# Bias bands read backwards from one 30 KB table, and four PSUM banks for products outside the attention

## The chip, the cores and the metric

The kernel runs on one core of a Trainium2 chip. Such a core has five engines that work side by side, each through its own list of instructions in order: TensorE (PE in the profile, its weight loads PEld), VectorE (DVE), ScalarE (ACT), GpSimd (POOL) and SyncE (SP), and 16 DMA engines that all queues share. The metric is the device time of one execution in microseconds, as the median of several runs. Lower is better.

## The reference, cut to what matters

A trunk of two layers works on 256 positions of 1024 columns, all in float32. Each layer adds half of a gated FFN (2816 wide), an attention of three branches whose gated results are summed and projected, half of a second FFN, and a last gated term.

```
for i in range(DEPTH):
    h = h + 0.5 * swiglu(rms_norm(h, g0), ffn1_wi[i], ffn1_wo[i])
    n = rms_norm(h, g1); q, k, v, gates of the branches = split_cols(n @ w_in[i], IN_SPLITS)
    ya = diff_attention(...)         # 4 heads of two score maps each, causal
    yb = nsa_attention(...)          # 8 heads: compressed blocks, selected blocks, window
    yc = swa_sink_attention(...)     # 8 heads, window of 128, with sinks
    h = h + (sum of sigmoid(gate) * (y @ w_branch)) @ w_out[i]
    h = h + 0.5 * swiglu(rms_norm(h, g2), ffn2_wi[i], ffn2_wo[i])
    h = h + sigmoid(rms_norm(h, g3) @ w_ple_gate[i]) * (p[i] @ w_ple[i])
return rms_norm(h, final_norm)
```

All three branches add a bias to the scores that depends on the distance between query and key alone: `rel_bias[rel_bucket(dist)]`, one column for each of 20 heads, with 32 buckets for distances up to 128. Where a key may not be seen, the score is -1e30.

## The kernel before, in words

Each product of float32 matrices is made of three matmuls of a shorter format: a left side and a weight are each split into a high part and the rest (`mul3`, lines 220 to 222: high by high, high by rest, rest by high). Weights come as a stream of chunks of 128 x 1024 (512 KB). SyncE fetches a chunk into one of four `raw` buffers (line 263), ScalarE copies it to the high part `wh` (line 213), and VectorE subtracts to get the rest, `wl` (line 208). Six buffers hold split chunks. A chunk of an FFN product covers two of the eight 128-row steps of the sum.

A product (`product`, lines 290 to 305) runs over two halves of 128 positions, t = 0 and 1, with one PSUM bank each (128 x 512), the second half some steps behind the first. When a half is done its `done` function empties the bank. The program writes the work in this order, and a scheduler then places the instructions of each engine by priority and by its own idea of time; buffers and banks that share a tag (`mm`, `s`, `tp`, `y`) are handed out in turn, and an instruction that needs one waits until the last reader of its previous content is done.

The eight banks are: two `mm` for products, two `s` for attention scores, three `tp` for transposes, one `y`.

In the first FFN of the program there are 11 products of gate and up columns (tiles ff; in the order the third is ff_354 and ff_406 before, ff_353 and ff_405 after). `done` applies Silu on ScalarE (line 458) and multiplies on VectorE into `gated` (line 459): after that the bank is free. Every second product the result is cut into 16-bit halves (`cut`, line 426), turned by DMA (`flip`, line 427), put together (`whole`, line 432) and split (gT).

Beside this FFN the program makes its constants (`setup`). One matmul and an addition give `tb`, the bias of 20 heads at 384 distances, with -1e30 where the mask forbids (line 1060). GpSimd writes it to `table` in DRAM (line 1061) and copies it 128 times, to `rev` (line 1062). A band is a tile of 128 queries x 4 heads x 256 distances in which each query's row is shifted by one place; `rev_band` reads it with a row step of one element less than a row of `rev` (line 1035). GpSimd reads two bands for the compressed branch, from which eight small copies make `cbias` (lines 1086 and 1087); SyncE reads five bands a layer for the attention. There line 529 adds a band to the scores and takes the maximum in one VectorE instruction:

```
nc.vector.tensor_tensor_reduce(out=p[j], in0=ps[j], in1=bias[j], scale=-1.0, scalar=low,
                               op0=ALU.add, op1=ALU.min, accum_out=st[:, j:j + 1])
```

Of the kernel before, what the change touches and what calls it, by code (L numbers as in the profile page):

```python
# [134 lines left out]

def _constants():
    u = np.arange(REV)
    dist = 255 - u
    n = np.maximum(dist, 0)
    nf = np.maximum(n, 1).astype(np.float32)  # L140
    big = 16 + (np.log(nf / np.float32(16)) / np.float32(math.log(MAXDIST / 16)) * np.float32(16)).astype(np.int32)
    bucket = np.where(n < 16, n, np.minimum(big, BUCKETS - 1))
    onehot = (bucket[None, :] == np.arange(BUCKETS)[:, None]).astype(np.float32)
    dead = np.zeros((NB, REV), np.float32)
    dead[:, dist < 0] = NEG
    dead[12:, dist >= 128] = NEG
    ql, t, m = np.arange(128)[:, None, None], np.arange(2)[None, :, None], np.arange(16)[None, None, :]
    cmask = ((128 * t + ql - 16 * m - 31 >= 0) & (m < 15)).astype(np.float32).reshape(128, 32)
    return {"onehot": onehot, "dead": dead, "cmask": cmask, "ident": np.eye(128, dtype=np.float32),
            "fold": np.tile(np.eye(32, dtype=np.float32), (2, 1))}  # L150
# [28 lines left out]
def trunk(ctx: ExitStack, tc: tile.TileContext, a: dict, out: bass.AP, index: list):  # L179
# [10 lines left out]

    def mm_bank(name):
        return bank("mm", 2, name)

    def tp_bank(name):
        return bank("tp", 3, name)
# [94 lines left out]
    def product(lhs, nk, done, name, w, skew=SKEW):  # L290

        def run():
            ps = [None] * NT
            for step in range(nk + skew):
                for t, k in ((0, step), (1, step - skew)):
                    if 0 <= k < nk:
                        wh, wl = w(k)
                        if k == 0:
                            ps[t] = mm_bank(f"{name}{t}")
                        xh, xl = lhs(t, k)  # L300
                        mul3(ps[t][:, :w.width], xh, xl, wh, wl, k == 0, k == nk - 1)
                        if k == nk - 1:
                            done(t, ps[t])
                        flow.tick()
        return run
# [182 lines left out]
    def attention(i, norm, after):  # L488
# [3 lines left out]
        def begin():  # L492
            nonlocal pool
            pool = phase("attn")
            for t in range(NT):
                merged[t] = pool.tile([128, D], F32, name=f"merged{t}")

# [56 lines left out]

        def band(first):
            b = pool.tile([128, 4, 256], F32, tag="band", bufs=2, name="band")
            rev_band(b, first)
            return b

        def y_tile(name):  # L560
# [20 lines left out]
        def attend_a():  # L581
            bnd = band(0)

            def first(u):
                m, t = u
                nk = 128 * (t + 1)
                s = scores("s", qk[m], [0, 1], t, lambda x, r, k: qk[m][r, x, 2 + k, :nk])
                yield
                p = pool.tile([128, 4, 256], F32, tag="p", bufs=3, name="p")
                st = None  # L590
                for st in softmax([p[:, j, :nk] for j in range(4)], [s[j // 2][:, j % 2, :nk] for j in range(4)],
                                  [bnd[:, 2 * m + j % 2, 256 - nk:] for j in range(4)]):
                    yield
                nc.vector.reciprocal(st[:, 8:12], st[:, 4:8])
                nc.vector.tensor_scalar(st[:, 10:12], st[:, 10:12], nlam[:, i:i + 1], None, op0=ALU.mult)
                for x in range(2):
                    nc.vector.tensor_scalar(p[:, 2 + x, :nk], p[:, 2 + x, :nk], st[:, 10 + x:11 + x], None, op0=ALU.mult)
                    nc.vector.scalar_tensor_tensor(p[:, x, :nk], p[:, x, :nk], st[:, 8 + x:9 + x], p[:, 2 + x, :nk],
                                                   op0=ALU.mult, op1=ALU.add)
                yield  # L600
                return p
# [191 lines left out]
        def attend_b():  # L793
            bnd, y_ps = {}, {}

            def first(u):
# [3 lines left out]
                if t == 0:  # L800
                    p = pool.tile([128, 4, 2, 128], F32, tag="p", bufs=3, name="p")
                    s = scores("s", qB[0], [2 * g, 2 * g + 1], 0, lambda x, r, m: kB[0][r, x, g:g + 3:2, :128])
                    rows = [(j, k) for j in range(4) for k in range(2)]
                    pr = [p[:, j, k] for j, k in rows]
                    sr = [s[j // 2].rearrange("p m (k n) -> p m k n", k=2)[:, j % 2, k] for j, k in rows]
                    br = [bnd[g][:, j, 128:] for j, k in rows]
                else:
                    p = pool.tile([128, 4, 256], F32, tag="p", bufs=3, name="p")
                    s = scores("s", qB[0], [2 * g, 2 * g + 1], 1, lambda x, r, m: kB[0][r, x, 2 * ss[0] + g, :])
                    pr = [p[:, j] for j in range(4)]  # L810
                    sr = [s[j // 2][:, j % 2] for j in range(4)]
                    br = [bnd[g][:, j] for j in range(4)]
                n = len(pr)
                yield
                st = None
# [48 lines left out]
        def attend_c():  # L864
# [4 lines left out]
            def first(u):  # L869
# [7 lines left out]
                sink = nsink[:, i, 4 * g:4 * g + 4]  # L877
                pr = [p[:, j, :nk] for j in range(4)]
                st = None
                for st in softmax(pr, [s[j // 2][:, j % 2, :nk] for j in range(4)], [bnd[g][:, j, 256 - nk:] for j in range(4)], sink):  # L880
                    yield
                sub(st[:, 8:12], st[:, 0:4], sink)
                nc.scalar.activation(st[:, 8:12], st[:, 8:12], AF.Exp)
# [89 lines left out]
        yield compress  # L973
        yield from branch(2, yC)
        yield from branch(1, yB, True)
        for c in range(2):
            yield product(lambda t, k: (mT[t][:, 0, k, :], mT[t][:, 1, k, :]), NK, after(c), "wo", streamed(i, f"wo{c}", 512))

# [46 lines left out]
    sg = base.tile([128, DEPTH], F32, name="sg")  # L1025
    cbias = base.tile([128, NT, 8, 16], F32, name="cbias")
    table = dram.tile([1, NB * REV], F32, name="table")
    rev = dram.tile([128, NB * REV], F32, name="rev")

    def rows(src, steps):  # L1030
        return bass.AP(tensor=src.tensor, offset=src.offset, ap=[[0, 128]] + steps)

    def rev_band(b, first, queue=nc.sync):
        ap = rev[:, :]
        queue.dma_start(b, bass.AP(tensor=ap.tensor, offset=ap.offset + first * REV + 127,
                                   ap=[[NB * REV - 1, 128], [REV, 4], [1, 256]]))

    def fetched_late(queue, *args):
        tc.keep_in_program_order(queue.dma_start(*args))
# [1 line left out]
    def setup(pool):  # L1041
# [17 lines left out]
        tb = pool.tile([NB, REV], F32, name="tb")  # L1059
        nc.vector.tensor_tensor(tb, tb_ps[:NB, :REV], dead, op=ALU.add)  # L1060
        nc.gpsimd.dma_start(table[0, :].rearrange("(n u) -> n u", n=NB), tb)
        nc.gpsimd.dma_start(rev, table.to_broadcast([128, NB * REV]))
        nc.gpsimd.memset(cbias, NEG)
        nc.vector.tensor_scalar(nsink, nsink, -1.0, None, op0=ALU.mult)
        lv = lamp.rearrange("p l (a b d) -> p (l a) b d", a=2, b=2)
# [11 lines left out]
        bands = []  # L1077
        for g in range(2):
            b = pool.tile([128, 4, 256], F32, tag="band", bufs=2, name="band")
            rev_band(b, 4 + 4 * g, nc.gpsimd)  # L1080
            bands.append(b.rearrange("p (par pr) c -> p par pr c", par=2))
        yield
        for g, b in enumerate(bands):
            for par in range(2):
                o = cbias.rearrange("p t (g pr par) n -> p t g par pr n", g=2, par=2)
                tc.keep_in_program_order(nc.vector.tensor_copy(o[:, 0, g, par, :, 0:7], b[:, par, :, 159:256:16]))
                tc.keep_in_program_order(nc.vector.tensor_copy(o[:, 1, g, par, :, 0:15], b[:, par, :, 31:256:16]))
        yield

    opened = []  # L1090
# [81 lines left out]
```

## Time and profile before

| | us |
|---|---|
| median of 3 runs (1371.64 to 1373.06) | 1372.09 |
| the profiled execution, its own time | 1372.78 |
| its span, first to last instruction | 1371.0 |
| TensorE busy (98%) | 1341.5 |
| VectorE busy (69%) | 944.7 |
| ScalarE busy (57%) | 779.4 |
| weight chunks of 512 KB, issue to landing, median | 4.4 |
| the copy rev<-table, 3840 KB | 18.3 |

The profile is of one execution. "Busy" counts the time in which an engine has an instruction under way, so a matmul that is followed closely by the next overlaps it and the sum says nothing on pace; the number of matmuls in a stretch does. A row's idle time is put down to what ended it. The wait of an engine matters where it delays the engine that ends last.

### The profile page before, as it was taken

The page shows a single profiled execution, that of the slowest core. Times are in us where ns is not written, and L with a number is a line of the kernel's source. Part 1 is how long each engine was busy: PE and PEld are TensorE (multiplying, and loading weights), DVE is VectorE, ACT ScalarE, POOL GpSimd, SP SyncE. Part 2 cuts the span into 40 slices and gives each one's busy share as a digit, 9 for nine tenths or more (in the row PEclk, how much of TensorE's full clock was granted, in tenths as well). Part 3 has the DMA queues.
Part 4 walks back from the last instruction along what each step waited for, and adds up shares of the span by engine and source line. Part 5 has one row for each costly group of instructions (what it writes and reads, how often), then busy time and mean ns, then how long its engine had stood idle before and what let it go on. Part 6 is the DMA issues. An engine that isn't in the chain of part 4 may idle for free.

```text
span 1371.0 us, 18293 instructions
## 1 busy us (share of the span) xinstructions
PE 1341.5 (98%) x6454; PEld 1098.2 (80%) x6454; DVE 944.7 (69%) x1779; ACT 779.4 (57%) x1378; POOL 19.0 (1%) x37
## 2 busy tenths in 40 slices
PE   8988999999999999999999999999999999999997
PEld 6766888887787788888888888888887778888886
DVE  7546656777886766766677665667697776776665
ACT  7435445668766455545665444566785656455454
POOL 0000000000000000000000000000000000000000
PEclk9999999999999999999999999999999999999999
DMA  8797757444653467775657885754547435777662
GB/s 306 199 265 227 216 177 237 142 152 156 215 175 109 153 189 213 215 210 192 203 189 219 223 226 171 235 170 137 162 151 232 127 122 168 216 222 218 194 202 84
DMA packets 121993, 261.07 MB, mean 190 GB/s; under 512 B 56816, under 2 KB 62372, under 8 KB 121774
## 3 DMA queue, kind: packets, MB, share of 16 engines
q1 hardware_dynamic: 121006, 254.34, 60.3%
q0 software_dynamic: 464, 5.01, 1.2%
q8 instruction: 50, 0.82, 0.2%
q10 hardware_dynamic: 432, 0.56, 0.1%
q14 instruction: 41, 0.34, 0.1%
HBM read 247.26 MB, written 5.01 MB: 184 GB/s over the span
## 4 chain that ended last, share of the span: by engine, by line
PE 88%; DMA 5%; DVE 3%; ACT 2%; issue 1%; SPq 0%; POOLq 0%; POOL 0%; DVEq 0%; ACTq 0%
PE ff L220 10%; PE ff L221 10%; PE ff L222 10%; PE fo L221 6%; PE fo L220 6%; PE fo L222 6%; DMA raw<-in_wst 4%; PE gate L220 3%; PE gate L221 3%; PE gate L222 3%; PE s L520 2%; PE A L220 2%; PE A L222 2%; PE A L221 2%; PE br L220 2%; PE br L222 2%
## 5 line engine op out<-in xcount | busy, mean ns | idle before, releaser
L208 DVE TENSOR_TENSOR wl<-raw,wh 128x1024 fp32r<-128x1024 f32 (+1 forms) x450 | 540.8, 1211 | 176.2 <-ACT wh L213 169.5
L213 ACT ACTIVATE wh<-raw 128x1024 fp32r<-128x1024 f32 (+1 forms) x450 | 469.4, 1049 | 227.7 <-PE fo L222 85.8
L220 PE MATMUL ff<-wh,nT 128*128 128x512 f32 x704 | 276.8, 395 | 13.0 <-DVE gated L459 8.4
L221 PE MATMUL ff<-wl,nT 128*128 128x512 f32 x704 | 276.2, 393 | 0.7 <-DVE wl L208 0.5
L222 PE MATMUL ff<-wh,nT 128*128 128x512 f32 x704 | 275.0, 391 | 0.0
L220 PEld LDWEIGHTS ff<-wh,nT 128*128 128x128 f32 x704 | 133.2, 189 | 45.6 <-DVE gated L459 11.0
L221 PEld LDWEIGHTS ff<-wl,nT 128*128 128x128 f32 x704 | 133.3, 189 | 30.0 <-DVE wl L208 2.7
L222 PEld LDWEIGHTS ff<-wh,nT 128*128 128x128 f32 x704 | 133.3, 189 | 27.9
L221 PE MATMUL fo<-wl,gT 128*128 128x512 f32 x352 | 134.2, 392 | 0.0
L222 PE MATMUL fo<-wh,gT 128*128 128x512 f32 x352 | 133.7, 389 | 0.0
L220 PE MATMUL fo<-wh,gT 128*128 128x512 f32 x352 | 133.2, 390 | 0.0
L458 ACT ACTIVATE act<-ff,stats 128x256 f32<-128x256 f32 x88 | 41.4, 473 | 104.0 <-PE ff L222 103.9
L459 DVE TENSOR_TENSOR gated<-act,ff 128x256 f32<-128x256 f32 x88 | 36.6, 417 | 74.3 <-ACT act L458 74.3
L221 PE MATMUL gate<-wl,nT 128*128 128x512 f32 x192 | 77.5, 404 | 1.5 <-DVE wl L208 1.5
L220 PE MATMUL gate<-wh,nT 128*128 128x512 f32 x192 | 78.8, 410 | 0.0
L222 PE MATMUL gate<-wh,nT 128*128 128x512 f32 x192 | 77.3, 402 | 0.0
L220 PEld LDWEIGHTS fo<-wh,gT 128*128 128x128 f32 x352 | 66.1, 188 | 13.9
L222 PEld LDWEIGHTS fo<-wh,gT 128*128 128x128 f32 x352 | 66.1, 188 | 13.4
L221 PEld LDWEIGHTS fo<-wl,gT 128*128 128x128 f32 x352 | 66.1, 188 | 13.3
L213 ACT ACTIVATE gT<-whole 128x512 fp32r<-128x512 f32 (+1 forms) x48 | 28.3, 590 | 63.0 <-DVE whole L432 62.2
L531 ACT ACTIVATE p<-p,st 128x128 f32<-128x128 f32 (+1 forms) x128 | 56.8, 447 | 12.2 <-DVE st L529 12.0
L320 ACT ACTIVATE nT<-nt,ngt 128x128 fp32r<-128x128 f32 x112 | 32.0, 369 | 30.8 <-PE nt L228 30.8
(297 smaller groups left out, 2002.8 us busy)
## 6 DMA issues: line engine op xcount, KB each, us to landing
raw<-in_wst SPq DMA_DIRECT2D x438, 512.0 KB, 4.4
band<-rev SPq DMA_DIRECT2D x10, 512.0 KB, 4.1
rev<-table POOLq DMA_DIRECT2D x1, 3840.0 KB, 18.3
raw<-in_wbv SPq DMA_DIRECT2D x4, 420.0 KB, 3.0
flip<-cut SPq DMA_TRANSPOSE x96, 3.8
xt<-in_xt SPq DMA_DIRECT2D x4, 256.0 KB, 5.3
raw<-in_wst SPq DMA_DIRECT2D x4, 256.0 KB, 4.0
h<-in_x SPq DMA_DIRECT2D x2, 512.0 KB, 8.0
```

The source lines that it names most:

```text
L208: nc.vector.tensor_tensor(o, x, y, op=ALU.subtract)
L213: nc.scalar.activation(hi, src, AF.Copy)
L220: nc.tensor.matmul(ps, xh, wh, start=start, stop=False)
L221: nc.tensor.matmul(ps, xh, wl, start=False, stop=False)
L222: nc.tensor.matmul(ps, xl, wh, start=False, stop=stop)
L320: ins = nc.scalar.activation(T[:, 0, k + m, :], src[:, 128 * m:128 * m + 128], AF.Copy, scale=ngt[:, self.row, k + m:k + m + 1])
L458: nc.scalar.activation(act, ps[:, :256], AF.Silu, scale=norm.r(t))
L459: nc.vector.tensor_tensor(held[t][:, 256 * (f % 2):256 * (f % 2) + 256], act, ps[:, 256:], op=ALU.mult)
L520: nc.tensor.matmul(o, q[r, x, qb[m], t * 128:(t + 1) * 128], kk, start=x + y == 0, stop=x == 1)
L531: nc.scalar.activation(p[j], p[j], AF.Exp, bias=st[:, j:j + 1], scale=-1.0, accum_out=st[:, n + j:n + j + 1])
```

## The change: what it does

`dist` in the table now rises with the index instead of falling, `rev` and the DMA that fills it are gone, and `read_band` reads a band from the one row of `table`, with a row step of one element. Each query's row of a band so runs in the opposite direction, and `back` gives the readers a view with a step of -1 (for cbias -16) from the other end.

`product_bank` takes the place of `mm_bank` in `product`. While `wide[0]` is set, every second pair of halves takes a bank of tag `s` in place of `mm`. `wide[0]` is set at the start, cleared at the beginning of each attention and set again ahead of its last product, wo.

```
 def _constants():
     u = np.arange(REV)
-    dist = 255 - u
+    dist = u - 127
...
+    wide = [True, 0]
+
+    def product_bank(name):
+        wide[1] += 1
+        return bank("s" if wide[0] and wide[1] % 4 >= 2 else "mm", 2, name)
...
                         if k == 0:
-                            ps[t] = mm_bank(f"{name}{t}")
+                            ps[t] = product_bank(f"{name}{t}")
...
             pool = phase("attn")
+            wide[0] = False
...
-            rev_band(b, first)
+            read_band(b, first)
...
-                                  [bnd[:, 2 * m + j % 2, 256 - nk:] for j in range(4)]):
+                                  [back(bnd[:, 2 * m + j % 2], nk) for j in range(4)]):
...
-                    br = [bnd[g][:, j, 128:] for j, k in rows]
+                    br = [back(bnd[g][:, j], 128) for j, k in rows]
...
         yield from branch(1, yB, True)
+        yield lambda: wide.__setitem__(0, True)
         for c in range(2):
...
-    rev = dram.tile([128, NB * REV], F32, name="rev")
...
-    def rev_band(b, first, queue=nc.sync):
-        ap = rev[:, :]
-        queue.dma_start(b, bass.AP(tensor=ap.tensor, offset=ap.offset + first * REV + 127,
-                                   ap=[[NB * REV - 1, 128], [REV, 4], [1, 256]]))
+    def read_band(b, first, queue=nc.sync):
+        ap = table[:, :]
+        queue.dma_start(b, bass.AP(tensor=ap.tensor, offset=ap.offset + first * REV, ap=[[1, 128], [REV, 4], [1, 256]]))
+
+    def back(b, n, step=1):
+        return bass.AP(tensor=b.tensor, offset=b.offset + step * (n - 1), ap=list(b.ap)[:-1] + [[-step, n]])
...
         nc.gpsimd.dma_start(table[0, :].rearrange("(n u) -> n u", n=NB), tb)
-        nc.gpsimd.dma_start(rev, table.to_broadcast([128, NB * REV]))
...
-            rev_band(b, 4 + 4 * g, nc.gpsimd)
+            read_band(b, 4 + 4 * g, nc.gpsimd)
...
-                tc.keep_in_program_order(nc.vector.tensor_copy(o[:, 0, g, par, :, 0:7], b[:, par, :, 159:256:16]))
-                tc.keep_in_program_order(nc.vector.tensor_copy(o[:, 1, g, par, :, 0:15], b[:, par, :, 31:256:16]))
+                tc.keep_in_program_order(nc.vector.tensor_copy(o[:, 0, g, par, :, 0:7], back(b[:, par], 7, 16)))
+                tc.keep_in_program_order(nc.vector.tensor_copy(o[:, 1, g, par, :, 0:15], back(b[:, par], 15, 16)))
```

The scheduler places instructions anew. On TensorE, at the step from the second to the third product of the first FFN, before (ff_314 is the second half of the second product, ff_354 the first half of the third; what a row waits for stands in brackets, with PE, Activation and DVE for TensorE, ScalarE and VectorE):

```order
L220 MATMUL ff_314<-wh,nT 128x512
L221 MATMUL ff_314<-wl,nT 128x512
L222 MATMUL ff_314<-wh,nT 128x512
L220 MATMUL ff_354<-wh,nT 128x512 [waits DVE_49]
L221 MATMUL ff_354<-wl,nT 128x512
L222 MATMUL ff_354<-wh,nT 128x512
L220 MATMUL ff_354<-wh,nT 128x512
```

The same place after (ff_313 and ff_353 are the same halves; the lines are those of the changed file):

```order
L227 MATMUL ff_313<-wh,nT 128x512
L228 MATMUL ff_313<-wl,nT 128x512
L229 MATMUL ff_313<-wh,nT 128x512
L227 MATMUL ff_353<-wh,nT 128x512 [waits PE_49,Activation_49]
L228 MATMUL ff_353<-wl,nT 128x512 [waits DVE_49]
L229 MATMUL ff_353<-wh,nT 128x512
L227 MATMUL ff_353<-wh,nT 128x512
L228 MATMUL ff_353<-wl,nT 128x512
L229 MATMUL ff_353<-wh,nT 128x512
L227 MATMUL ff_353<-wh,nT 128x512 [waits Activation_49]
```

The half starts after one wait for VectorE before, and none of its further matmuls waits; after, it waits chunk by chunk, for the copy ahead of its first matmul and for the split ahead of its second.

On VectorE, around the sixth to eighth product of the first FFN, before (ff_643 and ff_695 are the sixth, ff_754 and ff_806 the seventh, ff_846 the eighth; tb stood ahead, behind ff_538 of the fifth):

```order
L459 TENSOR_TENSOR gated<-act,ff_695 128x256
L426 COPY cut<-gated 128x512 x2
L208 TENSOR_TENSOR wl<-raw,wh 128x1024 x4
L432 COPY whole<-flip 128x512 x2
L208 TENSOR_TENSOR gT_184<-whole,gT_184 128x512
L459 TENSOR_TENSOR gated<-act,ff_754 128x256
L432 COPY whole<-flip 128x512 x2
L459 TENSOR_TENSOR gated<-act,ff_806 128x256
L208 TENSOR_TENSOR gT_185<-whole,gT_185 128x512
L208 TENSOR_TENSOR wl<-raw,wh 128x1024 x6
L459 TENSOR_TENSOR gated<-act,ff_846 128x256
```

The same place after (ff_694 ends the sixth product, ff_752 and ff_804 are the seventh, ff_844 the eighth):

```order
L466 TENSOR_TENSOR gated<-act,ff_694 128x256
L1072 TENSOR_TENSOR tb<-tb,dead 20x384
L433 COPY cut<-gated 128x512 x2
L215 TENSOR_TENSOR wl<-raw,wh 128x1024
L439 COPY whole<-flip 128x512 x2
L215 TENSOR_TENSOR gT_183<-whole,gT_183 128x512
L466 TENSOR_TENSOR gated<-act,ff_752 128x256
L439 COPY whole<-flip 128x512 x2
L215 TENSOR_TENSOR wl<-raw,wh 128x1024
L215 TENSOR_TENSOR gT_184<-whole,gT_184 128x512
L215 TENSOR_TENSOR wl<-raw,wh 128x1024 x2
L466 TENSOR_TENSOR gated<-act,ff_804 128x256
```

The addition that makes tb moves behind the sixth product, and the groups of four and six splits ahead of the emptyings become groups of one to three.

On GpSimd, around the table, before:

```order
L340 TENSOR_TENSOR stats<-stats,mhalf 128x1 x2
L1061 DMA table<-tb 20x384
L1062 DMA rev<-table 128x7680
L1035 DMA band<-rev 128x4x256 x2
L340 TENSOR_TENSOR stats<-stats,mhalf 128x1
L728 MEMSET kbd 128x64
```

The same after:

```order
L347 TENSOR_TENSOR stats<-stats,mhalf 128x1 x2
L1073 DMA table<-tb 20x384
L1044 DMA band<-table 128x4x256 x2
L347 TENSOR_TENSOR stats<-stats,mhalf 128x1
L736 MEMSET kbd 128x64
```

One row is gone, and the bands stand right behind the table.

## Rows read from the trace of the kernel before

**Rows 1.** The page: TensorE's busy time, its slices in tenths, ff's first matmuls.
```profile
PE 1341.5 (98%) x6454; PEld 1098.2 (80%) x6454; DVE 944.7 (69%) x1779; ACT 779.4 (57%) x1378; POOL 19.0 (1%) x37
...
PE   8988999999999999999999999999999999999997
...
L220 PE MATMUL ff<-wh,nT 128*128 128x512 f32 x704 | 276.8, 395 | 13.0 <-DVE gated L459 8.4
```

**Rows 2.** Windows: length, engines' busy time (count), granted clock, DMA share, GB/s.
```profile
30.00:38.00 8.00, 5.60 (x18) 4.18 (x17) 5.59 (x9) 2.75 (x5) 0.00 (x0) 0.79 0.94 259
38.00:86.00 48.00, 48.00 (x210) 38.59 (x209) 28.45 (x51) 21.77 (x28) 1.28 (x2) 1.00 0.71 221
86.00:92.00 6.00, 2.63 (x10) 1.58 (x8) 0.95 (x1) 1.92 (x2) 1.54 (x2) 0.91 1.07 238
92.00:120.00 28.00, 21.92 (x79) 16.04 (x79) 17.96 (x25) 12.34 (x16) 0.00 (x0) 0.90 0.91 263
120.00:150.00 30.00, 30.00 (x134) 24.86 (x133) 22.93 (x35) 17.34 (x22) 0.00 (x0) 1.00 0.79 211
240.00:460.00 220.00, 217.17 (x1209) 177.33 (x1208) 171.82 (x419) 149.09 (x336) 2.78 (x4) 0.99 0.49 156
```

**Rows 3.** Groups of instructions from 0 to 125 us: busy, mean ns, idle before.
```profile
L220 PE MATMUL ff<-wh,nT 128*128 128x512 f32 x142 | 57.9, 417 | 13.0 <-DVE gated L459 8.4 <-ACT wh L213 3.9 <-ACT nT L320 0.7
```

**Rows 4.** Timeline of TensorE, waits in brackets: start, length, instruction.
```profile
32.91 0.80 PE L220 MATMUL ff<-wh,nT 128*128 128x512 f32 x1 [2.40 <-DVE gated L459]
...
91.07 1.22 PE L220 MATMUL ff<-wh,nT 128*128 128x512 f32 x2 [3.37 <-ACT wh L213]
...
113.94 0.50 PE L220 MATMUL ff<-wh,nT 128*128 128x512 f32 x1 [3.18 <-DVE gated L459]
```

**Rows 5.** Timeline of VectorE around two emptyings of a bank.
```profile
30.06 2.47 DVE L208 TENSOR_TENSOR wl<-raw,wh 128x1024 fp32r<-128x1024 f32 x2 [0.70 <-ACT wh L213]
32.44 0.75 DVE L459 TENSOR_TENSOR gated<-act,ff 128x256 f32<-128x256 f32 x2
...
104.20 5.03 DVE L208 TENSOR_TENSOR wl<-raw,wh 128x1024 fp32r<-128x1024 f32 x4 [2.53 <-ACT wh L213]
...
113.47 0.41 DVE L459 TENSOR_TENSOR gated<-act,ff 128x256 f32<-128x256 f32 x1
```

**Rows 6.** The chain of waits that ended last: start, length, what.
```profile
55.79 4.97 DMA lamp<-in_lamp
...
72.30 17.63 DMA raw<-in_wst
...
93.00 11.35 DMA raw<-in_wst
```

**Rows 7.** DMA issues: count, KB each, median us from issue to landing.
```profile
raw<-in_wst SPq DMA_DIRECT2D x438, 512.0 KB, 4.4
band<-rev SPq DMA_DIRECT2D x10, 512.0 KB, 4.1
rev<-table POOLq DMA_DIRECT2D x1, 3840.0 KB, 18.3
...
band<-rev POOLq DMA_DIRECT2D x2, 512.0 KB, 9.7
...
gfin<-in_gfin SPq DMA_DIRECT2D x1, 512.0 KB, 4.8
```

**Rows 8.** Timeline of SyncE and VectorE: a band's issue, and its first reader.
```profile
315.10 0.38 SPq L1035 DMA_DIRECT2D band<-rev  x1
...
334.78 0.28 DVE L529 CUSTOM_DVE_ANT_0 p<-s,band 128x128 f32<-128x128 f32 x1
```

**Rows 9.** Readers of a band: duration ns min/median/max, first and last start, forms.
```profile
L529 DVE CUSTOM_DVE_ANT_0 p<-s,band x96: 283/352/425, 247.8 to 1103.3; 128x128 f32<-128x128 f32 x48, 128x256 f32<-128x256 f32 x48
L529 DVE CUSTOM_DVE_ANT_0 p<-s,band,nsink x32: 343/416/487, 306.7 to 994.7; 128x128 f32<-128x128 f32 x16, 128x256 f32<-128x256 f32 x16
...
L1086 DVE COPY cbias<-band x4: 163/166/167, 187.3 to 187.8; 128x14 f32<-128x14 f32 x4
```

More of the change, by code (lines that the diff above doesn't have):

```diff
@@ L811, in first @@
                     sr = [s[j // 2][:, j % 2] for j in range(4)]
-                    br = [bnd[g][:, j] for j in range(4)]
+                    br = [back(bnd[g][:, j], 256) for j in range(4)]
                 n = len(pr)
@@ L879, in first @@
                 st = None
-                for st in softmax(pr, [s[j // 2][:, j % 2, :nk] for j in range(4)], [bnd[g][:, j, 256 - nk:] for j in range(4)], sink):
+                for st in softmax(pr, [s[j // 2][:, j % 2, :nk] for j in range(4)], [back(bnd[g][:, j], nk) for j in range(4)], sink):
                     yield
```

## The prediction

> **What bounds the kernel now.** I read the page first: TensorE is busy for 1341.5 us, 98% of the span, and the slices show that what is missing is missing at the start: 8s stand among the first slices, 9s in all others but the last [rows 1]. So the question is what the opening loses and why. Second view, the stretches of the first FFN, where nearly every instruction of TensorE is a matmul of 512 columns. At full pace 30 us hold 134, 4.47 a us or 0.224 us each. But 30 to 38 us hold 18, 86 to 92 us 10 and 92 to 120 us 79, with the DMA engines at 0.9 or more of their time and a granted clock of 0.79, 0.91 and 0.90, so that part of each runs at 1.2 in place of 2.4 GHz after a wait [rows 2]. The missing work in time: 35.7 - 18 = 17.7 matmuls or 4.0 us in the first stretch, 26.8 - 10 = 16.8 or 3.8 us in the second, 125.1 - 79 = 46.1 or 10.3 us in the third. That is 18.1 us, and no more is to be had there.
>
> Third view, who was waited for. All 13.0 us of waiting that the page has for the first matmul of each three of ff [rows 1] lie before 125 us: 8.4 us on `gated`, the VectorE instruction that empties a product's PSUM bank, and 3.9 us on the weights [rows 3]. The three FFNs that follow have none. TensorE's timeline gives the single waits: 2.40 and 3.18 us on `gated`, 3.37 us on a weight copy of ScalarE [rows 4].
>
> Fourth view, VectorE at those places. At 30.06 us two weight splits (2.47 us) stand ahead of `gated`; ahead of the one at 113.47 stand six, of which four already take from 104.20 to 109.23 [rows 5]. So a wait for a bank is here a wait for weights once removed: TensorE can't start the product whose weights are split, because the bank is emptied behind the splits of later weights.
>
> Fifth view, the chain of waits: 17.63 us from 72.30 for one weight chunk and 11.35 us from 93.00 for another [rows 6], where the median is 4.4 us. Beside the first runs `rev<-table`, 3840 KB in 18.3 us; beside the second the two bands that GpSimd issues, 9.7 us each, against 4.1 us for the ten others [rows 7].
>
> **The change part by part.**
>
> *The copy goes.* One DMA of 3840 KB leaves GpSimd's queue, and the bands follow `table` at once. The chunk issued at 72.30 was wanted when TensorE ran dry, at 91.07 - 3.37 = 87.7 us; at the median of 4.4 us it lands 11 us before that. So the 3.8 us go. What is late next is the bands, 2 x 512 KB as before, which now meet full buffers. Bounds for what stays of the 10.3 us: nothing, as in 38 to 86 us, where the constants and lamp were fetched beside the weights and no matmul is missing (210 in 48 us, DMA share 0.71 [rows 2]); or all of it. The nearest row is that stretch: 0.29 of the DMA time is free, and four chunks are in flight or waiting ahead of use. I take 2 us.
>
> *Four banks.* While `wide` is set, products use the two banks of the scores too, so that a product needn't wait for the one before to be emptied. The order shows the first matmul of the third product waiting for one tick of VectorE before, and for the copy and the split of its own first chunk now. Its fourth chunk is split by 31.3 us, the first of the two splits at 30.06; the second is of the next product. So the 2.40 us go, and the slow clock behind them: 4.0 us. The wait before 113.94 is inside the 10.3 us. Latest after this are the splits, and VectorE's order has three at most between two emptyings where it had six. Behind the attention (wo, the second FFN, the last gate) `wide` is set again, but no wait for `gated` is there to remove: nothing. Should the freed banks only bring the weights' own wait forward, the gain is 0, the other bound.
>
> *Bands from the table.* Size, shape and the 512 runs of 1 KB stay; the source shrinks to four spans of 1.5 KB. Nearest rows for one place read again and again: lamp, 256 KB out of 2 KB, 4.97 us [rows 6]; gfin, 512 KB out of 4 KB, 4.8 us; and the copy itself, 3840 KB out of 30 KB at 210 GB/s [rows 7]. All run at the common pace. Bounds: 4.1 us as now, and 9.7 us as GpSimd's in the crowd. A band in the attention is issued at 315.10 and first read at 334.78 [rows 8], which covers both, so I take nothing there. If that cover went, each band would hold up its attention by what it lands late.
>
> The Trainium skill has a rule against this part: DMA: Bandwidth & Descriptors, section Latency and other measured facts, tells of copies with row pitches at large powers of two that fall to about half their rate and suspects streams that meet on one HBM channel. A pitch of 4 bytes would be that suspicion at its worst. By these rows lamp and gfin, which repeat even fewer bytes, don't show it; a band from so narrow a source no run here shows. By the rule a band would land at half pace, which is the second rival.
>
> *Reading backwards.* 128 score additions and eight small cbias copies [rows 9] take one operand with a step of -1 or -16. No row has a negative step. From the ends of the first form, 283 ns for 128 columns and 425 for 256, a column costs 1.1 ns and the rest is fixed. Bounds: 0, and, at twice the price a column, 64 x 128 x 1.1 + 64 x 256 x 1.1 ns = 27 us on VectorE, 13.5 a layer. Beside it: in 240 to 460 us VectorE is busy 171.8 of 220 us [rows 2], so 48 us are free. I take nothing, as the forward row is already one column a pass; without the cover half of it, some 13 us, would come through. A gain has no reason.
>
> *What moves.* `tb` stands behind the second half of the sixth product on VectorE in place of the first half of the fifth (the order's second piece), so that `table` is written 72 x 0.224 = 16 us later in the work, some 12 us later on the clock. Its first reader outside GpSimd's own two bands is the cbias copy at 187.3 us [rows 9], 100 us away. The bands of GpSimd then land near 90 us. In the late attention and in wo the order shifts too. The slices hold 9s there [rows 1], so there is little to win; I count 0 and put 2 us either way into the range.
>
> **Sum**, against the profiled execution's own 1372.78 us (its span of 1371.0 and 1.8 around it): 3.8 + 10.3 - 2 + 4.0 = 16.1 us less, 1356.7 us. The median of the three runs lies 0.7 us below that execution: 1356 us.
>
> **The rivals.**
>
> *The second half stays* (0.16). Bands and flips drain the weights for as long as before. For it: a DMA share of 0.91 in that stretch and 9.7 us for a band. Against: the buffers now are full when it begins. 1372.1 - (18.1 - 10.3) = 1364.3 us.
>
> *The bands crawl* (0.06). At half pace the two of the first FFN take 19.4 us instead of 9.7, as long as the copy took. The starvation comes a little later and whole, and only the third product's bank wait goes: 1372.1 - 4.0 = 1368.1 us. Against it lamp and gfin. This is what the skill's channel suspicion would do here.
>
> *Reading backwards is slow* (0.06), the other side. Place: line 529, in both attentions. At four times the price a column VectorE gets 3 x 13.5 = 40 us more in a layer, 212 of 220 us busy, and as one queue it holds up the weight splits too. If half reaches TensorE, 40 us in all: 1396 us. It decides once the loss passes 16 us, with the same half from 2.2 times the price. For it: no row has a negative step. Against: the forward price is 1.1 ns, so nothing clever is there to lose.
>
> *Nothing comes of it* (0.04). Parts of the above and the new order cancel to within 0.2%, 2.7 us, about what a measurement of this kernel can tell from no change: 1372 us.
>
> **How the numbers follow.** The forecast holds 0.68. Its own range is 1352 (all 18.1 us, and 2 from the order) to 1361 (7 us stay). The first two rivals are on its side: faster 0.68 + 0.16 + 0.06 = 0.90; same 0.04; slower 0.06. From 1352 to 1366 us lie nearly all of the forecast and of the first rival, over 0.8.
>
> **What would show it.** Right: no `rev`; near 150 matmuls in 86 to 120 us and near 35 in 30 to 38, at full clock; the wait on `gated` from 8.4 us to under 1; line 529 still 283 to 425 ns; SyncE's bands at about 4 us. The first step fails if TensorE waits for weights once the bands are issued, the second if the wait at 30 us only changes its name to a split. If line 529 takes over 400 ns for 128 columns, the sign of the forecast is in doubt; a new slow stretch in the late attention would say that the order weighs more than I gave it.

## The result, and the profile after

The changed kernel takes 1358.39 us (median of four runs, 1356.39 to 1358.72) against 1371.87 us for the kernel before on the same chip: 13.5 us less, a ratio of 0.9900 (95% interval 0.9883 to 0.9917). The profiled execution took 1358.67 us, 14.1 us less than the one of before.

The page of the changed kernel, busy time and slices, as in [rows 1]:

```profile
PE 1336.3 (98%) x6454; PEld 1097.6 (81%) x6454; DVE 942.7 (69%) x1779; ACT 779.3 (57%) x1378; POOL 18.9 (1%) x36
...
PE   9999999999999999999999999999999999999997
```

The stretches of [rows 2] in the changed kernel:

```profile
30.00:38.00 8.00, 8.00 (x37) 6.62 (x36) 6.27 (x12) 3.12 (x5) 0.00 (x0) 1.00 0.96 269
38.00:86.00 48.00, 44.85 (x183) 35.42 (x182) 32.46 (x55) 24.44 (x31) 0.71 (x1) 0.93 0.75 208
86.00:92.00 6.00, 6.00 (x28) 4.97 (x27) 4.58 (x7) 4.54 (x7) 1.95 (x2) 1.00 0.99 255
92.00:120.00 28.00, 28.00 (x125) 23.18 (x124) 18.15 (x27) 12.65 (x17) 0.00 (x0) 1.00 0.76 246
```

The three stretches that lost work are full: 37 matmuls for 18, 28 for 10, 125 for 79, all at full clock, or 4.3, 4.0 and 10.3 us gained at 0.224 us each. But 38 to 86 us, which was full, now holds 183 for 210: 27 x 0.224 = 6.0 us lost anew, with the granted clock at 0.93 over the stretch. With the 0.7 us of the first 20 us (62 matmuls for 59) that makes 13.2 of the 14.1 us. The remaining 0.9 us lies elsewhere and was not traced.

Where TensorE waits for ff's weights from 0 to 125 us, as in [rows 3], and the two waits of the new stall in its timeline:

```profile
L227 PE MATMUL ff<-wh,nT 128*128 128x512 f32 x162 | 63.2, 402 | 3.2 <-ACT wh L220 3.2
```

```profile
67.67 0.80 PE L227 MATMUL ff<-wh,nT 128*128 128x512 f32 x1 [2.51 <-ACT wh L220]
...
69.11 0.79 PE L228 MATMUL ff<-wl,nT 128*128 128x512 f32 x1 [0.64 <-DVE wl L215]
```

No wait for `gated` is left (8.4 us before). In its place TensorE waits 2.51 and 0.64 us for a copy and a split of weights; each of the matmuls shown then lasts 0.8 us, where the first one after a wait takes 0.50 at full clock ([rows 4], 113.94 us). The two waits make up all of TensorE's idle time in 38 to 86 us (48.00 - 44.85 us). VectorE's timeline ahead of it, and ScalarE's:

```profile
59.76 0.43 DVE L1079 TENSOR_TENSOR lprod<-lamp 128x256 f32<-128x256 f32 x1 [3.98 <-DMA lamp<-in_lamp]
```

```profile
62.73 0.63 ACT L220 ACTIVATE gT<-whole 128x512 fp32r<-128x512 f32 x1 [9.71 <-DVE whole L439]
63.38 1.28 ACT L1081 ACT_TABLE_LOAD   x1
...
64.90 1.28 ACT L465 ACT_TABLE_LOAD   x1
...
66.57 1.05 ACT L220 ACTIVATE wh<-raw 128x1024 fp32r<-128x1024 f32 x1
```

The weight copy that TensorE wants stands last in a queue. VectorE waits 3.98 us for `lamp`; behind that product stand `cut`, and through it `flip` and `whole`; ScalarE's gT waits for `whole`, and behind gT stand the Exp of lambda with two table loads, and only then `wh`. The Trainium skill (ScalarE: Activation LUTs, section What ACT_TABLE_LOAD costs) gives about 1283 ns for such a load, and the trace agrees with 1.28 us.

None of this is new in order. The kernel before has this chain's instructions in the same order on both engines, and its `wh` starts only 1.0 us later; there TensorE has no wait from 38 to 86 us:

```profile
60.79 0.43 DVE L1068 TENSOR_TENSOR lprod<-lamp 128x256 f32<-128x256 f32 x1 [2.39 <-DMA lamp<-in_lamp]
```

```profile
63.76 0.63 ACT L213 ACTIVATE gT<-whole 128x512 fp32r<-128x512 f32 x1 [5.76 <-DVE whole L432]
64.42 1.28 ACT L1070 ACT_TABLE_LOAD   x1
...
65.93 1.28 ACT L458 ACT_TABLE_LOAD   x1
...
67.60 1.05 ACT L213 ACTIVATE wh<-raw 128x1024 fp32r<-128x1024 f32 x1
```

What differs is TensorE, which now uses up the weights in hand some 4 us earlier.

The bands and their readers, as in [rows 7, 9]:

```profile
raw<-in_wst SPq DMA_DIRECT2D x438, 512.0 KB, 4.4
band<-table SPq DMA_DIRECT2D x10, 512.0 KB, 4.5
...
band<-table POOLq DMA_DIRECT2D x2, 512.0 KB, 6.8
```

```profile
L537 DVE CUSTOM_DVE_ANT_0 p<-s,band x96: 281/353/425, 234.4 to 1089.3; 128x128 f32<-128x128 f32 x48, 128x256 f32<-128x256 f32 x48
L537 DVE CUSTOM_DVE_ANT_0 p<-s,band,nsink x32: 344/415/486, 293.3 to 980.7; 128x128 f32<-128x128 f32 x16, 128x256 f32<-128x256 f32 x16
L1097 DVE COPY cbias<-band x4: 158/161/165, 173.8 to 174.3; 128x14 f32<-128x14 f32 x4
```

A band from the one table lands in 4.5 us (4.1 before), and reading with a step of -1 or -16 takes what it took forwards.

### The profile page after: what moved, and what is told of

Same layout as the page of the kernel before. It is cut to its first block, busy times and chain, and to the rows that moved or that the text cites. A ratio compares the mean times of both kernels' runs of the same rounds, so it can differ in the third digit from the quotient of the medians.

```text
span 1356.9 us, 18297 instructions
## 1 busy us (share of the span) xinstructions
PE 1336.3 (98%) x6454; PEld 1097.6 (81%) x6454; DVE 942.7 (69%) x1779; ACT 779.3 (57%) x1378; POOL 18.9 (1%) x36
## 4 chain that ended last, share of the span: by engine, by line
PE 90%; DVE 4%; DMA 3%; ACT 1%; issue 1%; SPq 0%; POOLq 0%; POOL 0%; DVEq 0%; ACTq 0%
PE ff L228 10%; PE ff L227 10%; PE ff L229 10%; PE fo L228 6%; PE fo L227 6%; PE fo L229 6%; PE gate L227 3%; PE gate L228 3%; PE gate L229 3%; PE s L528 2%; DMA raw<-in_wst 2%; PE A L228 2%; PE A L227 2%; PE A L229 2%; PE br L227 2%; PE br L228 2%
## 5 line engine op out<-in xcount | busy, mean ns | idle before, releaser
L227 PE MATMUL ff<-wh,nT 128*128 128x512 f32 x704 | 272.0, 392 | 3.2 <-ACT wh L220 3.2
L229 PE MATMUL ff<-wh,nT 128*128 128x512 f32 x704 | 274.3, 391 | 0.0
L439 DVE COPY whole<-flip 128x512 uint16<-128x512 uint16 (+1 forms) x96 | 38.0, 433 | 14.9 <-DMA flip<-cut 14.2
```

The costliest lines, as they stand in the source:

```text
L227: nc.tensor.matmul(ps, xh, wh, start=start, stop=False)
L229: nc.tensor.matmul(ps, xl, wh, start=False, stop=stop)
L439: tc.keep_in_program_order(nc.vector.tensor_copy(halves(whole)[:, :128 * m, w], flip[:, w, :m].rearrange("p a b -> p (a b)")))
```

## The experiments

Three questions stood open: does the gain come from both parts, as the sum had it; what makes the new stall; and what did the copy cost, its bytes or the wait for them? Each kernel was timed in five rounds beside the kernel before, whose median in the four groups was 1371.2, 1370.5, 1371.4 and 1371.2 us. Kernels of different groups are best compared by their ratios.

| kernel | us | ratio to before (95%) |
|---|---|---|
| bands from the table alone | 1356.95 | 0.9889 to 0.9917 |
| four banks alone | 1357.60 | 0.9898 to 0.9939 |
| whole change, lambda held back | 1353.38 | 0.9857 to 0.9885 |
| whole change and an unread copy | 1355.91 | 0.9879 to 0.9916 |
| bands alone and an unread copy | 1370.58 | 0.9988 to 1.001 |
| kernel before, tb held back | 1366.77 | 0.9964 to 0.9999 |
| bands alone, unread copy behind the bands | 1364.68 | 0.9946 to 0.9972 |
| bands alone, lambda held back | 1357.43 | 0.9885 to 0.992 |
| bands alone and half an unread copy | 1361.43 | 0.9907 to 0.9943 |
| lambda held back, and an unread copy | 1353.70 | 0.9842 to 0.9889 |
| whole change, lambda without lamp | 1353.87 | 0.9856 to 0.9891 |
| whole change, Exp of lambda held back | 1353.56 | 0.9847 to 0.9882 |

**Bands from the table alone.**

```
-        return bank("s" if wide[0] and wide[1] % 4 >= 2 else "mm", 2, name)
+        return bank("mm", 2, name)
```

> The change's bands from the table, without the extra banks: every product takes one of two PSUM banks, as before. Theory (the copy's removal and the banks are two separate gains, and the new stall at 64 to 74 us is an old wait for lamp that shows because TensorE now comes there 4 us earlier): the wait for a bank at 30 us is back (18 matmuls in 30 to 38 us, 4.0 us lost), TensorE comes late to 64 us and so most of the 6 us stall at 64 to 74 us is gone; 86 to 120 us stay full. That is 14 us less than before, 1358 us, and nearly the time of the whole change. Rival (the new stall comes from the changed order of VectorE's and SyncE's instructions, not from the lead): the 4.0 us at 30 us are lost and the stall of 6 us is there too, 1362 us.

Windows of that kernel:

```profile
30.00:38.00 8.00, 5.60 (x19) 4.20 (x18) 5.95 (x10) 2.75 (x5) 0.00 (x0) 0.79 0.94 251
...
60.00:70.00 10.00, 9.78 (x42) 6.97 (x41) 6.18 (x17) 5.17 (x7) 0.50 (x1) 1.00 0.70 222
...
92.00:120.00 28.00, 28.00 (x126) 23.14 (x125) 21.27 (x31) 15.65 (x21) 0.00 (x0) 1.00 0.87 244
```

1356.95 us, as the theory had it: the loss at 30 us is back, the stall after 64 us is gone, and the later stretch is full. This run alone doesn't tell the lead from the order, since without the banks `tb` and the order around it are as before too; the order of the stall's own chain is the same in both kernels, as shown above, and the runs on lambda below remove its links. Without the banks the change is worth as much as with them.

**Four banks alone.** The copy, `rev_band` and forward reading stay, and only `product_bank` and `wide` are added.

> The four banks alone: the 128-row copy is still made, bands are read from it and forwards. Theory: 30 to 38 us become full (4.0 us), but the lead of 4 us is given back at the wait for lamp near 64 us or, what is left, to the weights that the copy starves in 86 to 120 us, since these land when the DMA rings let them, not when TensorE is ready: 1370 to 1372 us. Rival (the gains add up): 1368 us.

```profile
60.00:70.00 10.00, 7.07 (x27) 5.12 (x26) 7.21 (x16) 7.41 (x10) 0.00 (x0) 0.85 0.60 159
...
92.00:120.00 28.00, 26.91 (x119) 21.97 (x118) 13.53 (x21) 10.02 (x13) 1.54 (x2) 1.00 1.10 282
```

Both expectations fell: 1357.6 us (1355.67 to 1364.37). The stall after 60 us is there, but the copy of 3840 KB now takes only 6 matmuls from 92 to 120 us, where it took 46. The trace is of the fastest of six runs, and two of the others took 1363.3 and 1364.4 us, so the copy doesn't pass as cheaply each time. Still the gains of the two parts are for the most part the same gain.

**The whole change and an unread copy.** The copy is issued again where it was, and nobody reads it.

```
         nc.gpsimd.dma_start(table[0, :].rearrange("(n u) -> n u", n=NB), tb)
+        nc.gpsimd.dma_start(rev, table.to_broadcast([128, NB * REV]))
```

> The whole change, and beside it the copy of the table to 128 rows again, in its old place ahead of GpSimd's two bands, which nobody reads. Theory (the copy cost what it did by its traffic, which holds up the weights in the DMA rings): weights take over 15 us again beside the copy, TensorE runs dry for some 10 to 14 us behind it, 1368 to 1372 us. Rival (what cost time was the wait for the copy, of the bands and what hangs on them): with no reader of the copy the time stays at 1358 to 1360 us.

**Bands alone and an unread copy.** The same line in the kernel with bands alone.

> Bands from the table, two banks as before, and the copy to 128 rows again, which nobody reads. Without the extra banks the program's order puts tb, and with it the copy, back to where the kernel before has it (near 71 us on the clock; in the run with four banks and an unread copy it began at 85 us and cost nothing), and gives SyncE four transposes in a row there. Theory (the copy costs 14 us when it runs from 71 us, in front of weights that TensorE will want, and nothing from 85 us on): 86 to 92 us holds some 10 matmuls and 92 to 120 us some 79, as before; 1370 us. Rival (an unread copy costs nothing, what cost was that bands and cbias waited for it): 1357 us.

With four banks the unread copy costs nothing (1355.9 us), so the theory's number fell and the rival's is nearest; with two it costs all (1370.6 us), though nobody waits for it, so the rival's reason falls too. It is the copy's traffic that cost, or what it does to the queues beside it, and something that the banks bring along decides whether it does. GpSimd's and SyncE's timelines of the kernel before, around the copy:

```profile
71.47 0.56 POOL L1062 DMA_DIRECT2D rev<-table  x1 [1.51 <-DMA table<-tb]
```

```profile
75.70 16.59 SPq L427 DMA_TRANSPOSE flip<-cut  x4
92.38 23.10 SPq L263 DMA_DIRECT2D raw<-in_wst  x11
```

Four transposes in a row hold SyncE for 16.6 us, 12.1 of them on the second alone, and no weight chunk is issued from 75.2 to 92.4 us, though a split that ended at 82.5 us had freed a buffer. The group of their instructions, of before and of the changed kernel (ns, shortest, median and longest):

```profile
L427 SPq DMA_TRANSPOSE flip<-cut x10: 1194/1268/12131, 61.6 to 119.4; - x10
```

```profile
L434 SPq DMA_TRANSPOSE flip<-cut x12: 1194/1214/1342, 60.6 to 121.7; - x12
```

One transpose took 12.1 us to issue beside the copy, where 1.2 is usual; in the kernel with bands and an unread copy one took 13.5. With four banks the scheduler puts `tb` later, so that the copy begins near 85 us in place of 71. That suggested the moment as the cause, and two runs tried it.

**The kernel before, with tb held back.**

```
-        nc.vector.tensor_tensor(tb, tb_ps[:NB, :REV], dead, op=ALU.add)
+        tc.keep_in_program_order(nc.vector.tensor_tensor(tb, tb_ps[:NB, :REV], dead, op=ALU.add))
```

> The kernel before with one edit: the addition that makes tb is held back in VectorE's order to the row that it has in the changed kernel, one and a half products later, so that the copy begins near 85 us. Copy, bands, two banks and everything else stay. Theory (the moment of the copy decides): 86 to 120 us become full or nearly so, the 4.0 us at 30 us stay lost, the wait for lamp stays covered; 1357 us, the whole gain of the change without either of its parts. Rival (the four banks themselves let TensorE run through the copy): still starved, 1371 us.

```profile
86.00:92.00 6.00, 6.00 (x28) 4.99 (x27) 4.93 (x8) 4.79 (x7) 0.63 (x2) 1.00 0.96 284
92.00:120.00 28.00, 23.73 (x95) 18.54 (x94) 12.20 (x18) 8.93 (x13) 1.54 (x2) 0.94 1.06 290
```

1366.8 us, in runs from 1360.9 to 1376.2: between the two, so neither number came, and the gain is barely clear of noise. The loss from 86 to 92 us is gone, a part of the later one stays. TensorE runs dry at 105.4 us, and ScalarE's next weight copy shows why:

```profile
105.34 1.06 ACT L213 ACTIVATE wh<-raw 128x1024 fp32r<-128x1024 f32 x1 [7.57 <-DMA raw<-in_wst]
```

In the kernel with four banks alone the same copy comes at 103.48 us, and TensorE doesn't wait for it:

```profile
103.48 1.06 ACT L220 ACTIVATE wh<-raw 128x1024 fp32r<-128x1024 f32 x1 [6.08 <-DMA raw<-in_wst]
```

So it looks like a race. The copy lasts 16 to 22 us, and few weights land beside it: in the kernel with four banks alone no chunk lands between 88.3 and 103.4 us. What would count then is how much work TensorE has in chunks issued by the copy's start. It can be counted from the trace as the chunks that SyncE has issued when the copy begins (a full one is 12 matmuls, each of the first four 6), less the matmuls begun (less 10 of warming up and of tb), at 0.224 us each. The last two columns are of the same, profiled execution:

| kernel | copy begins | chunks | matmuls | work ahead, us | matmuls in 86 to 120 us | time, us |
|---|---|---|---|---|---|---|
| before | 71.47 | 29 | 254 | 15.7 | 88 | 1372.8 |
| bands alone, unread copy | 72.38 | 29 | 254 | 15.7 | 104 | 1369.4 |
| the same, copy behind the bands | 74.73 | 30 | 261 | 16.8 | 116 | 1367.8 |
| before, tb held back | 87.99 | 36 | 321 | 19.5 | 122 | 1366.3 |
| whole change, unread copy | 85.11 | 36 | 314 | 21.1 | 152 | 1355.3 |
| lambda held back, unread copy | 82.99 | 36 | 312 | 21.5 | 151 | 1353.7 |
| four banks alone | 85.31 | 36 | 311 | 21.7 | 145 | 1355.7 |

The more work is ahead, the less is lost: nearly nothing from 21 us on, 14 us (by the medians) at 15.7. But the three kernels from 21 us on all have four banks and the other four have two, so the table doesn't tell the work ahead from another effect of the banks. One such effect is in the traces: with `tb` held back TensorE waits 2.74 us for `gated` at 120.32 us, and none of the three with four banks waits for a bank there. How much each gives back was not separated.

**Bands alone, the unread copy behind the bands.** The line stands behind the two `read_band` calls in place of ahead of them.

> As the kernel with two banks and an unread copy, but the copy is issued behind GpSimd's two bands, 1 to 2 us later (near 73 us). SyncE's order then has two weight chunks between the two pairs of transposes, where the kernel before has four transposes in a row. Theory (the moment decides: the copy's bytes stand in front of the weights, and a transpose can't be issued beside it): the chunks issued near 72 us still take over 12 us, 1366 to 1371 us. Rival (SyncE's order decides: the four transposes in a row kept weights from being issued for 17 us): most of the loss goes, 1358 to 1361 us.

SyncE's timeline there:

```profile
77.43 14.06 SPq L434 DMA_TRANSPOSE flip<-cut  x2
91.60 3.18 SPq L270 DMA_DIRECT2D raw<-in_wst  x2
```

1364.7 us: some 6 us of the 14 come back, less than SyncE's order would give by the rival, more than by the theory. Two transposes take 14 us here as well, 12.7 of them the second. The edit also moves the copy 2.4 us and lets one more chunk go ahead of it, so the 6 us aren't the order's alone. More than half of the loss stays. The trace is of the slowest of nine runs (1367.8 us) and shows less of the gain than the median.

**Bands alone and half an unread copy.** The copy fills `rev[0:64]` alone.

> Bands from the table, two banks, and an unread copy of 64 rows in place of 128, issued where the kernel before issues its copy (near 72 us). Theory (TensorE lives on the chunks that landed ahead of the copy, some 16 us of work at that point, and starves only when the copy takes longer): a copy of some 9 us is survived, 86 to 120 us are full or nearly full, 1357 to 1359 us. Rival (the copy's bytes cost their share wherever they run): half of 14 us is lost, 1364 us.

1361.4 us, between the two numbers expected: 4.5 us are lost against bands alone (3.0 by the ratios), for 13.6 with the whole copy (13.2). Half the bytes cost a quarter to a third, which fits a reserve that covers the start; it doesn't cover 10 us (what this copy took to land) wholly.

**Lambda held back.** `nsink`, the product of lamp, its sum, Exp and nlam move behind the cbias copies, the first two held there:

```
+        tc.keep_in_program_order(nc.vector.tensor_scalar(nsink, nsink, -1.0, None, op0=ALU.mult))
...
+        tc.keep_in_program_order(nc.vector.tensor_tensor(lprod, lv[:, :, 0, :], lv[:, :, 1, :], op=ALU.mult))
```

> The whole change, with the computation of lambda (the product of lamp, its sum, Exp and what follows, and the sinks' sign) held back in VectorE's and ScalarE's order until behind the cbias copies, some 100 us later; lamp is fetched when it was. Theory: VectorE no longer waits 3.98 us for lamp at 59.8 us, so the stall of TensorE at 64 to 74 us goes and 6 us come: 1352 us. Rival one (order or DMA traffic make the stall, not the wait for lamp): 38 to 86 us still hold some 183 matmuls, 1358 us. Rival two: the stall goes, but the lead is lost at a next wait before 120 us, 1356 to 1358 us.

```profile
60.00:70.00 10.00, 8.91 (x39) 6.83 (x38) 6.11 (x8) 5.37 (x7) 0.00 (x0) 1.00 0.88 235
```

1353.4 us, 5.0 us less than the change as it is (4.0 by the ratios), and the clock stays at 1.00.

**Bands alone, lambda held back.** The same edit without the extra banks.

> Bands from the table and two banks, with lambda's computation held back behind the cbias copies as in the run that gave 1353 us with four banks. Theory (the wait for lamp costs TensorE only where it comes there 4 us earlier, by the four banks): nothing or 0.3 us to win against the same kernel without the delay, 1356 to 1357 us. Rival (the wait for lamp is worth 5 us whatever TensorE's lead): 1352 us.

1357.4 us, no different from bands alone (1356.95), with runs from 1352.6 to 1360.2. So the stall costs only where TensorE comes 4 us earlier. Read the other way, the banks are worth some 1357.4 - 1353.4 = 4.0 us once the stall is out of the way.

**Lambda held back, and an unread copy.**

> The kernel of 1353 us (whole change, lambda's computation held back) with the unread copy of 128 rows in its old place ahead of the bands. Its tb stands five rows earlier in VectorE's order than in the changed kernel, so the copy begins near 81 us, with 36 chunks (408 matmuls) issued and TensorE at matmul 324, a reserve of 84 x 0.224 = 19 us. Theory (the reserve at the copy's start decides): it just suffices, as in the four-bank run with the copy, 1353 to 1356 us. Rival (in the four-bank runs with a copy it was the stall at 64 to 74 us that let the weights get ahead and so paid for the copy; without that stall the copy starves TensorE again): 5 us or more are lost, 1358 us and above.

1353.7 us against 1353.4: the rival's number falls. The trace still has a smaller stall (1.77 us of waiting for a split at 66.99 us, 193 matmuls in 38 to 86 us), so the copy isn't paid for by the stall of 6.0 us, but a kernel wholly without one was not tried.

**Lambda without lamp.** Lambda is made from zeros here, and lamp is not read:

```
-        nc.vector.tensor_tensor(lprod, lv[:, :, 0, :], lv[:, :, 1, :], op=ALU.mult)
+        nc.gpsimd.memset(lprod, 0.0)
+        tc.keep_in_program_order(nc.vector.tensor_tensor(lprod, lprod, lprod, op=ALU.mult))
```

> The whole change, but the product that begins lambda multiplies a tile of zeros in place of lamp (so lambda is a wrong constant; lamp is fetched all the same). Sum, Exp and the two table loads of ScalarE stay in the first FFN, three rows earlier at most. Theory (VectorE's wait of 3.98 us for lamp makes the stall): TensorE's stall at 64 to 74 us goes, 1353 us, as with everything held back. Rival one (ScalarE's two table loads of 1.28 us around the Exp, which stand between gT and the next weight copy, make it): the stall stays, 1358 us. Rival two (the wait of 2.93 us for the sinks at 52.8 us, which was moved away too in the run of 1353 us): the stall stays, 1358 us.

**Only the Exp held back.**

```
+        tc.keep_in_program_order(nc.scalar.activation(lam[:, 4:8], lam[:, 0:4], AF.Exp))
```

> The whole change, with only the Exp of lambda and what follows it held back behind the cbias copies: VectorE's product of lamp and its wait stay where they are, ScalarE's two table loads leave the first FFN. Theory (VectorE's wait for lamp): the stall stays but for the 2.56 us of table loads that stand in its way, of which at most all come, 1356 to 1358 us. Rival one (the table loads): the stall goes, 1353 us.

In the second kernel VectorE waits as long as ever; its timeline and TensorE's:

```profile
60.31 0.42 DVE L1079 TENSOR_TENSOR lprod<-lamp 128x256 f32<-128x256 f32 x1 [4.30 <-DMA lamp<-in_lamp]
```

```profile
66.83 0.51 PE L228 MATMUL ff<-wl,nT 128*128 128x512 f32 x1 [1.05 <-DVE wl L215]
```

Both give 1353.6 to 1353.9 us. The stall has two links in series, VectorE's wait (some 4 us) and ScalarE's detour for the Exp (2.56 us of table loads), and either one out is enough. In the second kernel 1.05 us of waiting for that split remain, 0.30 for the copy ahead of it, and the clock stays at 1.00. The first kernel takes out the wait, but with it the loads come earlier too (52.92 and 58.54 us), so it shows less cleanly what the wait alone is worth. Holding the Exp back is the smallest edit that beats both kernels: 1353.6 us, 0.9847 to 0.9882 of before. No run split the 6.0 us between waiting and slow clock; the two waits shown sum to 3.15 us, so by this estimate about half was the clock.

## Why the prediction was right, and where not

**The number** (1356 us forecast, 1358.4 measured, inside 1352 to 1366) came from a sum in which two terms were off: 2 us kept for the later stretch that went too, and no term at all for 38 to 86 us, where 6.0 us were lost. That the first, with small gains at the start and in the later stages that the sum didn't have, made up for some 4 of the 6.0 us is luck. Every sign of being right that the prediction named came true, and none of them looked at 38 to 86 us.

**The copy goes: right, and whole.** Forecast 3.8 + 10.3 - 2; both stretches are full, so the 2 us that were to stay went too. The mechanism was the copy's traffic and not the wait for what it makes, as argued; the run with two banks and an unread copy shows it. The prediction missed that SyncE itself was held, 16.6 us with transposes. How much of the loss comes from that and how much from chunks that land late no run separates.

**Four banks: right in place, wrong in what is late next.** The 4.0 us at 30 us came. The prediction named the splits as latest after it, and read 38 to 86 us, where nothing was missing [rows 2], as a stretch in which the constants and lamp cost nothing; so it put no term for it into the sum. That is the step that failed. A full stretch shows that the waits in it are covered, not that there are none: the wait for lamp stood in VectorE's queue before too (2.39 us), lamp's 4.97 us stood in the chain of [rows 6], and TensorE's 4 us delay was the cover. With the delay went the cover, and 6.0 us were lost.

**The sum treated the parts as independent.** Each alone gives the same 14 us. The banks, by the scheduler, move `tb`, and with it the copy, to where more weights are ahead; without the copy that move is worth nothing. Moving `tb` alone gave only some 4 us (1366.8), so the rest comes with the banks in some other way (2 us more work ahead, no wait for a bank behind the copy), which was not separated. "What moves: 0" was right for this change only because the copy left with it.

**Bands and reading backwards: right at nothing.** 4.5 us a band and 281 to 425 ns a reader. Nothing in the trace bears out the rivals built on them. The suspicion that the Trainium skill has (DMA: Bandwidth & Descriptors, section Latency and other measured facts) isn't borne out for this pattern: 512 KB out of four spans of 1.5 KB land in 4.5 us, nowhere near half pace.

**The second half stays** (1364.3 us) didn't happen: GpSimd's bands landed in 6.8 us, faster than the 9.7 of before.

## What to carry to other kernels

Before counting a removed wait as a gain, list the waits of the next stretch on every engine in order, covered ones too, and ask which of them the removed one was covering. A transfer's cost can depend on what the bottleneck has in hand when it begins, so a change made for another reason may be worth as much as removing the transfer, as four banks alone were here. And two changes that cure the same starvation must not be added up: time each alone.

## What the runs showed of the hardware

Beside a long copy from GpSimd's queue SyncE was held by a DMA transpose. The first of a group was issued in 1.2 to 2.6 us, the one behind it took 12.1, 13.5 and 12.7 us where the group came 3 to 4 us after the copy's start (before, bands alone with an unread copy, the same with the copy behind the bands), 4 to 7.3 us where it came 10 us and more after, and 7.6 us beside half the copy (median 1.2 to 1.3). Everything behind it in SyncE's queue stood as long. The Trainium skill (DMA: Bandwidth & Descriptors, section Issuing engines are not separate DMA queues) says that DMAs of all engines interleave on the same 16 DMA engines and that the time to initiate one is usually small; the first agrees, as chunks from SyncE took up to 20.3 us to land beside GpSimd's copy in place of 4.4, and the second doesn't hold for these transposes. Whether it is the transposes' own form or the amount of traffic ahead that holds them wasn't tried. VectorE read an operand with a step of -1 at the price of a forward one (281 and 425 ns for 128 and 256 columns, 283 and 425 before).
